# Two weight sums by accumulating loads, the residual by stores, and VectorE's order as written in memory attention

## The chip, the core and the metric

The kernel runs on one core of a Trainium2 chip. TensorE multiplies, VectorE (DVE) and ScalarE (ACT) work on tiles, GpSimd (POOL) and SyncE (SP) mostly issue transfers; each engine takes its own instructions, and semaphores order them against one another. The metric is the device time of one execution in microseconds (us).

## The reference

One layer of a streaming encoder in float32: 512 tokens of width 2048. A normalised input feeds one wide projection; its columns go to a gated short convolution, to latent attention with 16 heads, to cross-attention into 256 memory tokens with 4 heads of width 256, and to the gates. The three branches are projected, gated, merged, put through an output projection and added to the input:

```python
h = rms_norm(x, norm_g[l])
proj = h @ w_in[l]
...
o_conv = (conv_y * jax.nn.silu(conv_z)) @ w_conv_out[l]
...
o_mla = (mla_y * jax.nn.silu(mla_z)) @ w_mla_out[l]
mem_y = memory_attention(mem_q, mem, mem_norm_g[l], w_mem_kv[l], mem_qn_g[l], mem_kn_g[l])
o_mem = (mem_y * jax.nn.silu(mem_z)) @ w_mem_out[l]
merged = (jax.nn.sigmoid(g_conv) * o_conv + jax.nn.sigmoid(g_mla) * o_mla
          + jax.nn.sigmoid(g_mem) * o_mem)
x = x + merged @ w_o[l]
```

Memory attention is, for each head, a softmax over the 256 memory tokens of 512 queries and its product with the values.

## The kernel before

**Number format.** A float32 product is made of three matmuls: each operand is split into a high half (ScalarE copies it, `whi`, L281) and a low half (VectorE subtracts, `wlo`, L282), and `mm3` issues high by high (L161), high by low (L162) and low by high (L163). L163 is the only one that reads a weight's low half, so it is where TensorE waits for `wlo`.

**Panels.** The large projections are done in panels of two 128-column blocks with seven block products in place of eight (PRODUCTS). A panel takes four chunks of weights. A chunk is a 512 KB load of four 128x256 blocks into a `raw` tile of eight (`pair_weights`, four tiles in turn); VectorE then makes four more blocks, as sums: two at once (L276, 128x512), then one (L277) and one (L278), each from the one before; then come the two halves over seven blocks. One chunk feeds 42 matmuls of 256 columns. After the fourth chunk ScalarE copies one result and VectorE combines the products into the panel's four results (L318 to L327 in `panel_steps`), and `finish` does with them what the panel is for. The first two panels go alternately: chunks 0, 1, 2 of panel 0, then of panel 1, then chunk 3 of each.

**Preparation ahead.** `take()` hands the next chunk to the matmuls. `begin(at, stage)` moves a job of the queue on: stage 1 issues the load, 2 the adds, 3 the halves. With each `take`, the chunk itself and the next are brought to stage 3, the one after to stage 2, the one after that to stage 1. `fills` holds small pieces of other work, one run per `take`.

**What sets the order.** TensorE's order and SyncE's are as written. The other engines' order is set by a planner, except where VectorE is put under a manual schedule, and then it takes the instructions as they are written. Before, this holds from step 27 of the memory key and value projection until six panel steps of the input projection are through (`manual_dve`), and again around the turn into the output projection. Every engine takes its own queue in order.

**Places that the change touches.** The input projection begins at about 100 us. In memory attention (`mem_attend`, near 1650 to 1690 us) a head's 512 queries come in two halves; for each half TensorE makes scores, VectorE their maximum (L1152), ScalarE the exponentials with their sums (L1159), VectorE the reciprocals (L1162), and ScalarE scales (L1164). Then TensorE transposes the scaled tiles (L363), ScalarE and VectorE split them (`pt`), and TensorE multiplies with the values (`mv`). The keys of a head are split into `mk0h`, `mk1h` and the low halves. The four heads and other matmuls are interleaved by ORDER_MEM, a string of turns. The output projection takes the last 200 us: the merged branches come back from DRAM (`mg`), get sums and halves, and eight panels with the weights `w_o` end in `finish_o`, which loads the input block (`xr`), adds it on VectorE (L1350) and stores 256 KB from ScalarE's queue.

Of the kernel before, what the change touches and what calls it, by code (L numbers as in the profile page):

```python
# [30 lines left out]
P = 128  # L31
# [54 lines left out]
GATES.update({("gmem", _i): 16 + _i for _i in range(8)})  # L86

# [20 lines left out]
def body(ctx, tc, a, out):  # L108
# [110 lines left out]
    def pair_job(src):  # L219
        return lambda: pair_weights(src)  # L220
# [49 lines left out]
    def pair_weights(src):  # L270
# [3 lines left out]
        nc.sync.dma_start(flat(f[:, 0:4]), src)  # L274
        yield
        vec.tensor_tensor(out=f[:, 4:6], in0=f[:, 1:3], in1=f[:, 0:1].to_broadcast([P, 2, 256]), op=ALU.add)  # L276
# [53 lines left out]
    def panels(xp, weight, n, make, finish, first="acc", tail=None):  # L330
# [3 lines left out]
        order = [(0, c) for c in range(3)] + [(1, c) for c in range(3)] + [(0, 3), (1, 3)]  # L334
        order += [(i, c) for i in range(2, n) for c in range(4)]
        upcoming(*[pair_job(weight[i][c]) for i, c in order])
# [193 lines left out]
    work = panels(xp, a["w_h"], len(SEQUENCE), lambda n: make(n), lambda n, e: finish(n, e), "aux")  # L530
# [54 lines left out]
    begin(2, 2)  # L585
# [175 lines left out]

    def make(n):
        return etile(), None
# [57 lines left out]
    for _ in range(6):  # L821
        next(work)
# [15 lines left out]
    PLACES = ((2, 3), (6, 7), (4, 5), (0, 1))  # L838
# [292 lines left out]
    def mem_attend(head):  # L1131
# [11 lines left out]
        pr = []  # L1143
        for i2 in range(2):
# [16 lines left out]
            ri = pq.tile([P, 2], F32, tag="ri", name="ri", bufs=2)  # L1161
            vec.reciprocal(ri, sm)  # L1162
            for ii in range(2):
                act.activation(p[:, ii], p[:, ii], AF.Copy, scale=ri[:, ii:ii + 1])  # L1164
# [24 lines left out]
    run(ORDER_MEM, w=conv, **{str(n): m[n] for n in range(4)})  # L1189
# [99 lines left out]
    def sums_out(n):  # L1289
        pair_sums(mgs[n])  # L1290

    def split_out(n):
# [11 lines left out]
                 29: ((sums_out, 4),), 30: ((split_out, 4), (merged, 6)), 31: ((sums_out, 5),),  # L1304
                 32: ((split_out, 5),)}
# [9 lines left out]
    for tag, width in (("acc", 512), ("aux", 512), ("acc", 512), ("aux", 256), ("aux", 256)):  # L1315
        if done == 7:
            work = panels(xp, a["w_o"], 8, lambda n: make_o(n), lambda n, e: finish_o(n, e),
                          tail=lambda b, e: tail_o(b, e))
# [19 lines left out]
    def make_o(n):  # L1338
        def middle():
            xrs[n] = pe.tile([P, 2, S], F32, tag="xr", name="xr", bufs=2)  # L1340
# [110 lines left out]
```

## Time and profile before

| | us |
|---|---|
| median of three runs | 2166.34 (2165.52 to 2167.77) |
| the profiled execution | 2162.43 |
| its span in the trace | 2160.7 |
| TensorE matmuls busy | 2122.6 |
| VectorE busy | 1728.2 |
| ScalarE busy | 1010.8 |
| GpSimd busy | 130.9 |

The trace is of one execution. Its span begins at the first recorded instruction, and times below are counted from there. "Busy" is time in which an engine works on an instruction; the idle time of TensorE is the difference from the span. A wait is shown with the engine and line that ended it.

### The profile page before, as it was taken

The numbers are of one execution on the slowest core, as the hardware profiler recorded it, in microseconds if no ns is written. First come the engines' busy times: TensorE is split into PE (matmuls) and PEld (weight loads), VectorE is DVE, ScalarE is ACT, GpSimd is POOL, SyncE is SP. The second block draws the span as 40 slices with busy tenths as digits, with TensorE's granted clock in tenths as the row PEclk, the third lists the DMA queues.
The fourth block names the chain that finished last, engine by engine and source line by source line (L and its number), as shares of the span: only waits on it lengthen the run. The fifth ranks groups of instructions, "written<-read, shape, count | busy, mean of one in ns | idle before, by whom it ended". The sixth has DMA issues, their size and how long they took to land.

```text
span 2160.7 us, 38707 instructions
## 1 busy us (share of the span) xinstructions
PE 2122.6 (98%) x16040; PEld 2037.7 (94%) x16040; DVE 1728.2 (80%) x2740; ACT 1010.8 (47%) x1235; POOL 130.9 (6%) x189
## 2 busy tenths in 40 slices
PE   9989999999999999999999999999999999999899
PEld 7889999999999999999999999898988899987899
DVE  5986878888888888888878876788886688856886
ACT  6743444444444344344444444777765533323333
POOL 0000000000000000000000000212111100011000
PEclk9999999999999999999999999999999999999999
DMA  8634443333333333343444336222346957667443
GB/s 330 248 98 137 158 135 128 128 127 128 127 127 127 125 125 126 126 136 133 137 137 142 131 129 241 90 104 81 112 158 245 355 203 208 201 213 199 141 162 107
DMA packets 93441, 338.51 MB, mean 157 GB/s; under 512 B 10896, under 2 KB 11152, under 8 KB 91216
## 3 DMA queue, kind: packets, MB, share of 16 engines
q1 hardware_dynamic: 70848, 252.58, 34.5%
q0 software_dynamic: 13920, 59.51, 8.6%
q10 hardware_dynamic: 8496, 23.94, 3.1%
q8 instruction: 125, 2.05, 0.4%
q14 instruction: 52, 0.43, 0.1%
HBM read 273.34 MB, written 62.65 MB: 156 GB/s over the span
## 4 chain that ended last, share of the span: by engine, by line
PE 84%; DVE 5%; ACT 2%; DMA 2%; issue 1%; POOL 0%; DVEq 0%; ACTq 0%; POOLq 0%
PE acc L161 14%; PE acc L163 14%; PE acc L162 14%; PE aux L161 13%; PE aux L163 13%; PE aux L162 13%; DVE wlo L282 2%; PE aux L363 1%; PE aux L997 1%; DMA raw<-in_w_h 1%; ACT whi L281 1%; DVE raw L276 0%; PE aux L977 0%; PE aux L980 0%; PE aux L978 0%
## 5 line engine op out<-in xcount | busy, mean ns | idle before, releaser
L281 ACT ACTIVATE whi<-raw 128x1792 fp32r<-128x1792 f32 x304 | 517.6, 1703 | 795.6 <-PE aux L162 336.7
L282 DVE TENSOR_TENSOR wlo<-raw,whi 128x1792 fp32r<-128x1792 f32 x304 | 614.8, 2022 | 204.2 <-ACT whi L281 203.5
L163 PE MATMUL aux<-xp,wlo 128*128 128x256 f32 (+1 forms) x1712 | 479.8, 280 | 6.3 <-DVE wlo L282 6.2
L161 PE MATMUL aux<-xp,whi 128*128 128x256 f32 (+1 forms) x1712 | 480.4, 281 | 0.0
L162 PE MATMUL aux<-xp,whi 128*128 128x256 f32 (+1 forms) x1712 | 479.2, 280 | 0.0
L163 PE MATMUL acc<-xp,wlo 128*128 128x256 f32 x1680 | 470.2, 280 | 3.4 <-DVE wlo L282 3.4
L161 PE MATMUL acc<-xp,whi 128*128 128x256 f32 x1680 | 470.8, 280 | 0.0
L162 PE MATMUL acc<-xp,whi 128*128 128x256 f32 x1680 | 469.6, 280 | 0.0
L163 PEld LDWEIGHTS aux<-xp,wlo 128*128 128x128 f32 (+1 forms) x1712 | 321.1, 188 | 7.5 <-DVE wlo L282 7.5
L161 PEld LDWEIGHTS aux<-xp,whi 128*128 128x128 f32 (+1 forms) x1712 | 320.6, 187 | 0.0
L163 PEld LDWEIGHTS acc<-xp,wlo 128*128 128x128 f32 x1680 | 316.0, 188 | 4.6 <-DVE wlo L282 4.6
L162 PEld LDWEIGHTS aux<-xp,whi 128*128 128x128 f32 (+1 forms) x1712 | 320.2, 187 | 0.0
L161 PEld LDWEIGHTS acc<-xp,whi 128*128 128x128 f32 x1680 | 315.6, 188 | 0.0
L162 PEld LDWEIGHTS acc<-xp,whi 128*128 128x128 f32 x1680 | 315.1, 188 | 0.0
L276 DVE TENSOR_TENSOR raw<-raw 128x512 f32<-128x512 f32 x304 | 208.3, 685 | 36.5 <-DMA raw<-in_w_h 31.8
L155 DVE TENSOR_TENSOR wlo<-raw,whi 128x1024 fp32r<-128x1024 f32 (+2 forms) x89 | 100.5, 1131 | 75.1 <-ACT whi L154 72.7
L154 ACT ACTIVATE whi<-raw 128x1024 fp32r<-128x1024 f32 (+2 forms) x89 | 87.7, 986 | 101.4 <-PE acc L162 43.3
L278 DVE TENSOR_TENSOR raw<-raw 128x256 f32<-128x256 f32 x304 | 127.9, 422 | 6.3
L277 DVE TENSOR_TENSOR raw<-raw 128x256 f32<-128x256 f32 x304 | 127.9, 422 | 5.7
L161 PE MATMUL acc<-whi,blk 128*128 128x384 f32 (+1 forms) x224 | 84.2, 376 | 0.0
L356 POOL TENSOR_TENSOR rs_r<-rs_t,mhalf 128x2 f32<-128x2 f32 (+2 forms) x71 | 65.2, 929 | 276.7 <-DVE rs_t L355 217.2
L163 PE MATMUL acc<-whi,blk 128*128 128x384 f32 (+1 forms) x224 | 80.9, 361 | 0.0
(360 smaller groups left out, 3896.7 us busy)
## 6 DMA issues: line engine op xcount, KB each, us to landing
raw<-in_w_h SPq DMA_DIRECT2D x240, 512.0 KB, 3.5
raw<-in_w_mla_out SPq DMA_DIRECT2D x32, 512.0 KB, 4.2
raw<-in_w_o SPq DMA_DIRECT2D x32, 512.0 KB, 3.6
raw<-in_w_mem_kv SPq DMA_DIRECT2D x31, 512.0 KB, 7.4
gdram<-e ACTq DMA_DIRECT2D x22, 512.0 KB, 2.9
raw<-in_w_ukv SPq DMA_DIRECT2D x16, 512.0 KB, 4.3
raw<-in_w_conv_out SPq DMA_DIRECT2D x16, 512.0 KB, 8.3
aadram<-z POOLq DMA_DIRECT2D x8, 896.0 KB, 3.9
```

The source lines that it names most:

```text
L154: act.activation(hi[:, cols], raw[:, cols], AF.Copy)
L155: vec.tensor_tensor(out=lo[:, cols], in0=raw[:, cols], in1=r32(hi[:, cols]), op=ALU.subtract)
L161: nc.tensor.matmul(o, lhsT=s[0], rhs=m[0], start=start, stop=False, skip_group_check=shared)
L162: nc.tensor.matmul(o, lhsT=s[0], rhs=m[1], start=False, stop=False, skip_group_check=shared)
L163: nc.tensor.matmul(o, lhsT=s[1], rhs=m[0], start=False, stop=stop, skip_group_check=shared)
L276: vec.tensor_tensor(out=f[:, 4:6], in0=f[:, 1:3], in1=f[:, 0:1].to_broadcast([P, 2, 256]), op=ALU.add)
L277: vec.tensor_tensor(out=f[:, 6], in0=f[:, 5], in1=f[:, 1], op=ALU.add)
L278: vec.tensor_tensor(out=f[:, 7], in0=f[:, 6], in1=f[:, 3], op=ALU.add)
L281: act.activation(hi, f[:, 1:8], AF.Copy)
L282: vec.tensor_tensor(out=lo, in0=f[:, 1:8], in1=r32(hi), op=ALU.subtract)
L356: pool.tensor_tensor(out=r, in0=t, in1=mhalf[:, :n], op=ALU.pow)
L363: nc.tensor.transpose(out=b[:, i * P:(i + 1) * P], in_=s, identity=ident)
```

## The change

1. The first eight chunks of the input projection and of the output projection come as 768 KB loads, in which the host has put the first block twice more behind the four blocks; then GpSimd issues a DMA that adds 256 KB of the chunk onto these two (`accum_op`). For these chunks the VectorE instruction L276 is gone; L277 and L278 stay. This takes host arrays `w_h6` and `w_o6`.
2. Before the input projection, the third chunk is begun to stage 1, no longer to stage 2.
3. VectorE's written order holds through nine panel steps, no longer six; the `finish` of panels 0 and 1 runs as fills.
4. The residual: SyncE copies the first seven input blocks from DRAM to the output in DRAM during panels 12 to 18 of the input projection, and `finish_o` adds a panel's result there with one accumulating DMA of GpSimd (512 KB). Only the last panel keeps `xr`.
5. In `mem_attend` the scaling is split off (`scaled`): that of the first half comes after the exponentials of the second, that of the second half just ahead of the first transposes. ORDER_MEM runs with VectorE in its written order.
6. Two pairs of places for blocks in SBUF are swapped, and `split_out(5)` runs as a fill of the output panels.

The core of the diff:

```diff
+FIRST = [(0, c) for c in range(3)] + [(1, c) for c in range(3)] + [(0, 3), (1, 3)]
+SIX = 8
...
-    def pair_weights(src):
+    def pair_weights(src, six):
         f = raw_tile()
-        nc.sync.dma_start(flat(f[:, 0:4]), src)
-        yield
-        vec.tensor_tensor(out=f[:, 4:6], in0=f[:, 1:3], in1=f[:, 0:1].to_broadcast([P, 2, 256]), op=ALU.add)
+        if six is not None:
+            nc.sync.dma_start(flat(f[:, 0:6]), six)
+            nc.gpsimd.dma_start(flat(f[:, 4:6]), src[:, 256:768], accum_op=ALU.add)
+        else:
+            nc.sync.dma_start(flat(f[:, 0:4]), src)
+        yield
+        if six is None:
+            vec.tensor_tensor(out=f[:, 4:6], in0=f[:, 1:3], in1=f[:, 0:1].to_broadcast([P, 2, 256]), op=ALU.add)
         vec.tensor_tensor(out=f[:, 6], in0=f[:, 5], in1=f[:, 1], op=ALU.add)
         vec.tensor_tensor(out=f[:, 7], in0=f[:, 6], in1=f[:, 3], op=ALU.add)
...
-    work = panels(xp, a["w_h"], len(SEQUENCE), lambda n: make(n), lambda n, e: finish(n, e), "aux")
+    work = panels(xp, a["w_h"], len(SEQUENCE), lambda n: make(n),
+                  lambda n, e: fills.append(lambda: finish(n, e)) if n < 2 else finish(n, e), "aux",
+                  six=a["w_h6"])
...
-    begin(2, 2)
+    begin(2, 1)
...
     def make(n):
+        if n >= 12 and n < 19:
+            nc.sync.dma_start(out_rows(n - 12), a["xT"][:, n - 12].rearrange("p (f n) -> p f n", f=2))
...
-    for _ in range(6):
+    for _ in range(9):
         next(work)
     manual_dve.close()
...
+        def scaled(p, sm):
+            ri = pq.tile([P, 2], F32, tag="ri", name="ri", bufs=2)
+            vec.reciprocal(ri, sm)
+            for ii in range(2):
+                act.activation(p[:, ii], p[:, ii], AF.Copy, scale=ri[:, ii:ii + 1])
+                pr.append(p[:, ii])
...
-            ri = pq.tile([P, 2], F32, tag="ri", name="ri", bufs=2)
-            vec.reciprocal(ri, sm)
-            for ii in range(2):
-                act.activation(p[:, ii], p[:, ii], AF.Copy, scale=ri[:, ii:ii + 1])
-                pr.append(p[:, ii])
+            waiting.append((p, sm))
+            if i2 == 1:
+                scaled(*waiting[0])
             yield
         pts = []
         for j in range(2):
+            if j == 0:
+                scaled(*waiting[1])
...
-    run(ORDER_MEM, w=conv, **{str(n): m[n] for n in range(4)})
+    with tc.manual_schedule(engines={DVE}):
+        run(ORDER_MEM, w=conv, **{str(n): m[n] for n in range(4)})
...
     def finish_o(n, e):
-        fills.append(lambda: result(n, e))
...
-            vec.tensor_tensor(out=xr[:, f], in0=two(e)[:, f], in1=xr[:, f], op=ALU.add)
-            nc.scalar.dma_start(out[(2 * n + f) * P:(2 * n + f + 1) * P], xr[:, f])
+        nc.gpsimd.dma_start(out_rows(n), two(e), accum_op=ALU.add)
```

The order of TensorE's matmuls is the same before and after. In the changed kernel L276 to L278 are L288 to L290, L282 is L294, and L1164 is L1171.

**VectorE at chunks 6 to 8 of the input projection.** A `raw` number names one chunk's tile: counted from 0, raw_1208, raw_1261 and raw_1312 are chunks 6, 7 and 8 in both kernels, raw_1364 and raw_1428 are chunks 9 and 10 before, and raw_1489 is chunk 11 now. `e` is the panel's result tile. Before:

```order
L282 TENSOR_TENSOR wlo_1306<-raw_1208,whi_1305 128x1792
L276 TENSOR_TENSOR raw_1261<-raw_1261 128x512
L278 TENSOR_TENSOR raw_1364<-raw_1364 128x256
L277 TENSOR_TENSOR raw_1261<-raw_1261 128x256
L278 TENSOR_TENSOR raw_1261<-raw_1261 128x256
L276 TENSOR_TENSOR raw_1428<-raw_1428 128x512
L277 TENSOR_TENSOR raw_1428<-raw_1428 128x256
L282 TENSOR_TENSOR wlo_1358<-raw_1261,whi_1357 128x1792
L318 TENSOR_TENSOR e_1027<-aux_1029,e_1027 128x2x256
L278 TENSOR_TENSOR raw_1428<-raw_1428 128x256
```

Now:

```order
L294 TENSOR_TENSOR wlo_1357<-raw_1261,whi_1356 128x1792
L288 TENSOR_TENSOR raw_1312<-raw_1312 128x512
L289 TENSOR_TENSOR raw_1312<-raw_1312 128x256
L290 TENSOR_TENSOR raw_1312<-raw_1312 128x256
L330 TENSOR_TENSOR e_1025<-aux_1027,e_1025 128x2x256
L335 TENSOR_TENSOR e_1025<-aux_1028,e_1025 128x512
L288 TENSOR_TENSOR raw_1489<-raw_1489 128x512
L336 SCALAR_TENSOR_TENSOR e_1025<-aux_1028,e_1025 128x256
L338 TENSOR_TENSOR e_1025<-aux_1029,e_1025 128x256
L339 TENSOR_TENSOR e_1025<-aux_1029,e_1025 128x256
L294 TENSOR_TENSOR wlo_1414<-raw_1312,whi_1413 128x1792
```

Before, adds of chunk 10 (raw_1428) stood ahead of the low half of chunk 7 (raw_1261). Now the low halves of the first eight chunks have no later chunk's L276 ahead of them, and the combining of panel 0 stands whole ahead of the low half of the ninth chunk.

**ScalarE in memory attention**, from the exponentials of head 0 to the first scaling of the third head. `p` numbers name the halves: 18712, 18737, 18781, 18806 are 0A, 0B, 1A, 1B before; 18721, 18742, 18786, 18807 now. Before:

```order
L130 ACTIVATE mk0h_18894<-mkr_18890 128x256
L1159 ACTIVATE p_18712,sm_18711<-aux_18694,nm_18709,mqs_98 128x256 x2
L1159 ACTIVATE p_18737,sm_18736<-aux_18719,nm_18734,mqs_98 128x256 x2
L130 ACTIVATE mv_18682<-mvr_18680 128x512
L1164 ACTIVATE p_18712<-p_18712,ri_18715 128x256 x2
L1159 ACTIVATE p_18781,sm_18780<-aux_18763,nm_18778,mqs_98 128x256 x2
L130 ACTIVATE mv_18687<-mvr_18685 128x512
L1164 ACTIVATE p_18737<-p_18737,ri_18740 128x256 x2
L1159 ACTIVATE p_18806,sm_18805<-aux_18788,nm_18803,mqs_98 128x256 x2
L1164 ACTIVATE p_18781<-p_18781,ri_18784 128x256 x2
L130 ACTIVATE pt0_18833<-aux_18828 128x512
```

Now:

```order
L136 ACTIVATE mk0h_18903<-mkr_18899 128x256
L136 ACTIVATE mk1h_18907<-mkr_18899 128x256
L1190 ACTIVATE p_18742,sm_18741<-aux_18724,nm_18739,mqs_98 128x256 x2
L1171 ACTIVATE p_18721<-p_18721,ri_18745 128x256 x2
L136 ACTIVATE mv_18689<-mvr_18687 128x512
L136 ACTIVATE mv_18694<-mvr_18692 128x512
L1190 ACTIVATE p_18786,sm_18785<-aux_18768,nm_18783,mqs_98 128x256 x2
L1190 ACTIVATE p_18807,sm_18806<-aux_18789,nm_18804,mqs_98 128x256 x2
L1171 ACTIVATE p_18786<-p_18786,ri_18810 128x256 x2
L1171 ACTIVATE p_18742<-p_18742,ri_18829 128x256 x2
L136 ACTIVATE pt0_18838<-aux_18833 128x512
L136 ACTIVATE pt1_18846<-aux_18841 128x512
```

The scaling of 0B has moved from ahead of 1B's exponentials to behind them and behind the scaling of 1A.

**GpSimd in the output projection** (after; no row of L283 and L1378 stood there before):

```order
L1312 DMA mg_21723<-mgdram_117 128x1024
L283 DMA raw_21857<-in_w_o 128x512
L1319 DMA mgdram_117<-gt_21276 128x1024
L1312 DMA mg_21825<-mgdram_117 128x1024
L283 DMA raw_21893<-in_w_o 128x512
L283 DMA raw_21947<-in_w_o 128x512
L1312 DMA mg7_21880<-mgdram_117 128x1024
L283 DMA raw_22001<-in_w_o 128x512
L1378 DMA out_0<-e_21882 128x2x512
```

The accumulating loads of the weights stand between the stores (`mgdram<-gt`) and loads (`mg<-mgdram`) of the merge, in GpSimd's one queue.

More of the change, by code (lines that the diff above doesn't have):

```diff
@@ L328, in panel_steps, with panels @@
         yield
[L330 to L336, printed above, removed]
+    def panels(xp, weight, n, make, finish, first="acc", tail=None, six=None):
+        order = FIRST + [(i, c) for i in range(2, n) for c in range(4)]
+        upcoming(*[pair_job(weight[i][c], six[at] if six is not None and at < SIX else None)
+                   for at, (i, c) in enumerate(order)])
         tags = (first, "aux" if first == "acc" else "acc")
@@ L760, in body, with out_rows @@
     conv_e = {}
+    def out_rows(n):
+        return out[2 * n * P:2 * (n + 1) * P].rearrange("(f p) n -> p f n", f=2)
     def make(n):
+        if n >= 12 and n < 19:
+            nc.sync.dma_start(out_rows(n - 12), a["xT"][:, n - 12].rearrange("p (f n) -> p f n", f=2))
         return etile(), None
@@ L1143, in mem_attend @@
         pr = []
+        def scaled(p, sm):
[4 more added lines that the diff above has]
+                pr.append(p[:, ii])
+        waiting = []
         for i2 in range(2):
@@ L1303, in body @@
                  25: ((split_out, 3), (merged, 4), (merged, 5), (gate_load, 7)),
-                 29: ((sums_out, 4),), 30: ((split_out, 4), (merged, 6)), 31: ((sums_out, 5),),
-                 32: ((split_out, 5),)}
+                 29: ((sums_out, 4),), 30: ((split_out, 4), (merged, 6)), 31: ((sums_out, 5),)}
     late_blocks = []
@@ L1317, in body @@
             work = panels(xp, a["w_o"], 8, lambda n: make_o(n), lambda n, e: finish_o(n, e),
-                          tail=lambda b, e: tail_o(b, e))
+                          tail=lambda b, e: tail_o(b, e), six=a["w_o6"])
         banks = [bank(tag) for _ in range(width // P)]
@@ L1339, in middle @@
         def middle():
-            xrs[n] = pe.tile([P, 2, S], F32, tag="xr", name="xr", bufs=2)
-            nc.sync.dma_start(xrs[n].rearrange("p f n -> p (f n)"), a["xT"][:, n])
+            if n == 7:
+                xrs[n] = pe.tile([P, 2, S], F32, tag="xr", name="xr", bufs=1)
+                nc.sync.dma_start(xrs[n].rearrange("p f n -> p (f n)"), a["xT"][:, n])
         return pe.tile([P, 8, H], F32, tag="e", name="e", bufs=2), middle
     def finish_o(n, e):
-        fills.append(lambda: result(n, e))
-    def result(n, e):
-        xr = xrs[n]
-        for f in range(2):
-            vec.tensor_tensor(out=xr[:, f], in0=two(e)[:, f], in1=xr[:, f], op=ALU.add)
-            nc.scalar.dma_start(out[(2 * n + f) * P:(2 * n + f + 1) * P], xr[:, f])
+        nc.gpsimd.dma_start(out_rows(n), two(e), accum_op=ALU.add)
     def tail_o(b, e):
@@ L1367, in body @@
     merged(7)
-    fills += [lambda: None, lambda: sums_out(6), lambda: split_out(6), lambda: sums_out(7), lambda: split_out(7)]
+    fills += [lambda: split_out(5), lambda: sums_out(6), lambda: split_out(6), lambda: sums_out(7), lambda: split_out(7)]
     for n, _ in enumerate(work):
@@ L1437, in layout @@
     a["w_o"] = np.stack([halved(i["w_o"][0], c, c + P) for c in range(0, D, 256)])
+    for name in ("w_h", "w_o"):
+        first = np.stack([a[name][i][c] for i, c in FIRST[:SIX]])
+        a[name + "6"] = np.ascontiguousarray(np.concatenate([first, first[:, :, :256], first[:, :, :256]], axis=2))
     return a
```

6 lines of the change are left out of this document (3 added, 3 removed).

## The prediction, made before the changed kernel ran

> **What bounds the kernel now.** I read the busy shares first, then the busy time by stretch of the span, then what TensorE waited for. The columns of the second view are: stretch, length, then busy time of TensorE's matmuls, its weight loads, VectorE, ScalarE and GpSimd, the granted clock, the DMA share and GB/s.
>
> ```profile
> PE 2122.6 (98%) x16040; PEld 2037.7 (94%) x16040; DVE 1728.2 (80%) x2740; ACT 1010.8 (47%) x1235; POOL 130.9 (6%) x189
> ```
> ```profile
> 20.00:114.00 94.00, 91.57 (x449) 76.20 (x447) 75.18 (x94) 67.89 (x89) 6.26 (x8) 1.00 0.78 284
> 114.00:155.00 41.00, 33.83 (x275) 32.61 (x276) 34.55 (x42) 16.18 (x13) 0.00 (x0) 1.00 0.28 90
> 155.00:1160.00 1005.00, 1003.88 (x8512) 1003.02 (x8511) 835.29 (x1174) 422.57 (x327) 14.62 (x20) 1.00 0.40 131
> 1650.00:1690.00 40.00, 37.38 (x202) 31.06 (x202) 27.75 (x57) 27.52 (x70) 6.26 (x12) 0.96 0.71 254
> 1945.00:2050.00 105.00, 93.27 (x612) 83.83 (x611) 83.25 (x111) 37.57 (x30) 8.34 (x13) 1.00 0.57 171
> 2050.00:2150.00 100.00, 100.00 (x852) 100.00 (x851) 82.15 (x110) 35.98 (x25) 0.00 (x0) 1.00 0.42 143
> ```
>
> TensorE is the bound: of 2160.7 us it is idle for 38.1, and no edit here takes a matmul away. The idle time sits in spots: 41.00 − 33.83 = 7.2 us at the start of the input projection and 105.00 − 93.27 = 11.7 at the turn into the output projection. In the long stretches between (1.1 us idle in 1005, none in the last 100 us of output panels) VectorE has slack, and work taken from it buys nothing. So the question is only what the edits do to these spots, and whether they open new ones.
>
> TensorE's waits (engine, line, releaser; total us, times, longest), of the stretches 20 to 170, 1945 to 2050 and 1650 to 1690 us:
>
> ```profile
> PE aux L163 <- DVE wlo L282: 5.4, 3, 3.0
> PE acc L163 <- DVE wlo L282: 3.4, 4, 1.4
> ...
> PE acc L163 <- DVE wlo L282: 9.8, 7, 2.6
> PE aux L163 <- DVE wlo L282: 1.0, 4, 0.2
> ...
> PE aux L363 <- ACT p L1164: 2.4, 3, 1.7
> ```
>
> The first spot waits 8.8 us and the second 10.8 us for the low half of a weight chunk (wlo), the last of five operations on a chunk; the third spot, memory attention, waits 2.4 us for a scaled softmax tile. These 22 us are what the change can touch.
>
> **Input projection.** The costs of one chunk, and VectorE's own timeline where it goes wrong (start us, duration, then idle before it and the releaser):
>
> ```profile
> L281 ACT ACTIVATE whi<-raw 128x1792 fp32r<-128x1792 f32 x304 | 517.6, 1703 | 795.6 <-PE aux L162 336.7
> L282 DVE TENSOR_TENSOR wlo<-raw,whi 128x1792 fp32r<-128x1792 f32 x304 | 614.8, 2022 | 204.2 <-ACT whi L281 203.5
> L276 DVE TENSOR_TENSOR raw<-raw 128x512 f32<-128x512 f32 x304 | 208.3, 685 | 36.5 <-DMA raw<-in_w_h 31.8
> L278 DVE TENSOR_TENSOR raw<-raw 128x256 f32<-128x256 f32 x304 | 127.9, 422 | 6.3
> ```
> ```profile
> 142.47 0.69 DVE L276 TENSOR_TENSOR raw<-raw 128x512 f32<-128x512 f32 x1 [3.01 <-DMA raw<-in_w_h]
> 143.20 0.42 DVE L277 TENSOR_TENSOR raw<-raw 128x256 f32<-128x256 f32 x1
> 143.54 2.02 DVE L282 TENSOR_TENSOR wlo<-raw,whi 128x1792 fp32r<-128x1792 f32 x1
> ...
> 149.13 0.69 DVE L276 TENSOR_TENSOR raw<-raw 128x512 f32<-128x512 f32 x1 [1.84 <-DMA raw<-in_w_h]
> ```
>
> A chunk is 42 matmuls, at 1003.88 us / 8512 = 0.118 us each 4.95 us of TensorE, against 0.69 + 2 × 0.42 + 2.02 = 3.55 us of VectorE. The chunk rate is no trouble; the wlo of 143.54 was late because VectorE takes its queue in order and stood 3.01 us at a later chunk's L276, whose data had not landed. That cost TensorE the longest wait, 3.0; the 1.84 at 149.13 does the same once more.
>
> The change takes eight L276 away (8 × 0.685 = 5.5 us of VectorE), begins chunk 2's adds after wlo of chunk 1, and keeps VectorE's written order through nine panel steps, so wlo of chunks 6 and 7 no longer stands behind later chunks' adds. Walking the queue with the durations above: of the seven waits, those at chunks 1, 5, 6 and 7 (counted from 0) go and about 1 us stays at chunks 2 and 4. But the same written order now puts the combining of panel 0 (about 3 us: two 128x512 forms, three 128x256, and a copy) after wlo(7) and ahead of wlo(8), and the combining of panel 1, the scaling of panel 0 and the adds of two further chunks ahead of wlo(9). Panel 0 ends with chunk 6. Counted from there, wlo(8) is ready about 5.6 us later where chunk 8 asks at 5.1 (late by 0.5), and wlo(9) at 13 to 15 where chunk 9 asks at 10.5 (late by 2.5 to 4.5); chunk 10 then waits about 1. So 8.8 goes down to about 5 or 6; a wait also sits in gaps this view doesn't name (41.00 − 33.83 is 7.2 us in one stretch alone). I take **−5**; bounds −8.8 (nothing new waits) and 0 (the new waits equal the old).
>
> **Its price: two landings in series.** GpSimd adds 256 KB of the chunk into the loaded tile, which can start only when the 768 KB load has landed; L277 then waits for GpSimd's queue. An accumulating load is not in the trace. The nearest rows (KB of one transfer, median us from issue to landing):
>
> ```profile
> raw<-in_w_h SPq DMA_DIRECT2D x240, 512.0 KB, 3.5
> mgdram<-sg POOLq DMA_DIRECT2D x8, 512.0 KB, 5.6
> mgdram<-gt POOLq DMA_DIRECT2D x8, 512.0 KB, 6.3
> mgdram<-kn POOLq DMA_DIRECT2D x4, 256.0 KB, 9.5
> ```
>
> The rows of 5.6 and 6.3 are accumulating stores, twice the bytes; the last is GpSimd's slowest plain one. From below a plain load's 3.5 bounds it, from above 9.5. I take 6. A slot of the four raw tiles comes free at wlo(n − 4): 3.5 + 6 + 0.85 (L277, L278) + 1.70 (whi) + 2.02 (wlo) = 14.1 us, within 4 × 4.95 = 19.8. So it is hidden, until the accumulation alone takes 19.8 − 8.1 = 11.7. The Trainium skill ("DMA: Bandwidth & Descriptors", rules for kernel authors) says that an accumulating transfer must wait for the earlier one's semaphore, because nothing holds the bytes between its read and its write; so the landings cannot overlap, which the sum above has by the kernel's own wait, and no run so far shows an accumulating load.
>
> **Output projection.** Eight more L276 leave, 5.5 us, and in the second spot four of the L1350 adds (128x512, as L276: 2.7 us); split_out(5) moves from the tail of the merge to a panel's fill. VectorE is busy 83 of 105 us there, in order, and 10.8 us are waits for wlo. Removed work can cut at most 8.2 of it. Not all arrives: the remaining chunks' L288 (the former L276) still stands ahead of earlier wlo, waiting for loads, as at 142.47; and here the eight accumulations lie in GpSimd's queue behind merge stores and loads. I take **−6**, bounds −8.2 and 0. The other ten of the 14 adds, the ScalarE stores and seven input loads lie under 100 us of full TensorE (the row of 2050): 0. Should that cover fail, it is 10 × 0.685 = 6.9 us of VectorE more in hand, never less. The seven DRAM-to-DRAM copies (512 KB) fall in stretches at DMA share 0.40: 0.
>
> **Memory attention.** Here nothing is removed; the written VectorE order and the deferred scaling move work. ScalarE and TensorE before:
>
> ```profile
> 1655.49 0.42 ACT L130 ACTIVATE mk0h<-mkr 128x256 fp32r<-128x256 f32 x1 [2.35 <-PE aux L163]
> ...
> 1656.18 0.55 ACT L1159 ACTIVATE p<-aux,nm,mqs 128x256 f32<-128x256 f32 x1
> ...
> 1658.34 0.63 ACT L130 ACTIVATE mv<-mvr 128x512 fp32r<-128x512 f32 x1
> 1658.86 0.91 ACT L1164 ACTIVATE p<-p,ri 128x256 f32<-128x256 f32 x2
> 1659.66 0.56 ACT L1159 ACTIVATE p<-aux,nm,mqs 128x256 f32<-128x256 f32 x1
> ...
> 1661.27 0.91 ACT L1164 ACTIVATE p<-p,ri 128x256 f32<-128x256 f32 x2
> ...
> 1664.90 0.93 ACT L1164 ACTIVATE p<-p,ri 128x256 f32<-128x256 f32 x2
> 1665.70 1.07 ACT L154 ACTIVATE whi<-raw 128x1024 fp32r<-128x1024 f32 x1
> 1666.64 1.09 ACT L130 ACTIVATE pt<-aux 128x512 fp32r<-128x512 f32 x2
> ...
> 1682.00 0.56 ACT L1159 ACTIVATE p<-aux,nm,mqs 128x256 f32<-128x256 f32 x1
> ```
> ```profile
> 1659.42 0.73 PE L363 MATMUL aux<-ident,p 128*128 128x128 f32 x2 [0.18 <-ACT p L1164]
> 1661.83 1.17 PE L363 MATMUL aux<-ident,p 128*128 128x128 f32 x6 [1.68 <-ACT p L1164]
> ...
> 1664.98 2.05 PE L363 MATMUL aux<-ident,p 128*128 128x128 f32 x8
> ...
> 1681.55 1.03 PE L363 MATMUL aux<-ident,p 128*128 128x128 f32 x8
> ```
>
> Call the softmax halves of head h hA and hB. ScalarE's queue was: mk (head 3), exps 0A and 0B, scale 0A, exps 1A, scale 0B (1661.27), exps 1B, scale 1A, two pt, scale 1B. Now 0A's exps come before mk, but mk still waits for head 1's scores at 1655.49, with 0B's exps behind it (1656.2 to 1657.3), then scale 0A, two mv (0.6 each at most), four exps (0.55 each), scale 1A, and only then 0B: 1657.3 + 0.9 + 1.2 + 2.2 + 0.9 = 1662.5 for its start, against 1661.27. Head 0's transposes wait about 1 us longer. Scale 1B now stands behind 0B (0.9), two pt (1.1), a weight half (1.07) and two mv (1.2): 1662.5 + 4.3 = 1666.8 and, as the second pt waits for head 0's late transposes, rather 1667.5, against 1664.90; head 1's transposes at 1664.98 wait about 3. Scale 2B moves behind head 3's four exps (the last at 1682.00) and scale 3A: about 1683.4, where TensorE asked at 1681.55 and did not wait; and by VectorE's order head 3's maxima stand behind head 1's products, so 2 to 4.5. Sum: +6 to +8.5. I take **+8.5**, since each wait also delays the queue that the next one stands in; bounds 0 (ScalarE's slack absorbs it) and +10.
>
> **The clock.** In two stretches TensorE ran at half clock:
>
> ```profile
> 171.69:175.10 3.41, 3.41 (x18) 3.41 (x18) 2.70 (x7) 0.00 (x0) 0.54 (x1) 0.50 0.64 231
> 1663.31:1666.72 3.41, 3.41 (x12) 2.44 (x11) 1.44 (x3) 3.41 (x8) 0.00 (x0) 0.50 0.43 163
> ```
>
> Each loses half of 3.41 = 1.7 us, after a wait of 1.7 beside transposes. Three longer waits could bring one or two more (+1.7 to +3.4), fewer waits at 170 could take one away; I put +1.5. The Trainium skill ("TensorE: Matmul & The Clock Gate", Part 1 and "Why this matters for your kernels") wants no idle gap above about 3 us, and its Part 4 has transposes not counted as busy. The trace agrees with the second more than with the first, having a gated window after a gap of 1.7. By the first alone the clock term would be about 0, by both together up to +3.4, which speaks against this change.
>
> **The sum** is −5 − 6 + 8.5 + 1.5 = −1. The profiled execution took 2162.43 us (span 2160.7, 1.7 around it), 3.9 below the median of 2166.34. 2162.4 − 1 = 2161.4, and with the same 3.9 the median comes to **2165.3**, no change that can be measured: 0.2%, or 4.3 us, is about what a measurement of this kernel can tell.
>
> **The rivals.**
> - *Memory attention stays cheap.* If ScalarE takes 0B and 2B where the data is ready, as its 47% share would let it were its queue not fixed, the +8.5 falls to +1 and the clock term to 0: −5 − 6 + 1 = −10, 2156. For it: 27.5 of 40 us busy on ScalarE, so there is room. Against: the queue is in order, and 0B's exps were held by mk already at 1655.49. Chance 0.27, with mixtures below −4.3.
> - *The accumulating loads land late (slower).* Place: L289, the former L277, in VectorE's in-order queue. It decides from 11.7 us of landing, above the 9.5 of the slowest row. At 16 us a cycle of four chunks takes 24.1 for 19.8, 1.1 per chunk; four chunks at each projection are paced so (the first four are prefetched): +8.6, or 2174. For it: one GpSimd queue that also waits for merge loads, and the first 114 us at a DMA share of 0.78. Against: both accumulating rows are near 6. Chance 0.13.
> - *Memory attention at its bound with two more half-clock windows*, and the projections at half their gains: +10 + 3.4 − 5.5 = +7.9, 2174. It decides where each wait of 3 us falls inside one window. For it: the row of 1663.31. Against: both gains must fail at once. Chance 0.10.
> - *The edits don't act* (L289 and L288 take the place of L276, wait for wait; the new order is as good as the old): 0, 2166; within the forecast.
>
> **How the numbers follow.** The forecast, −4.3 to +4.3 with its middle at −1, gets 0.50; of it 0.02 falls out above and 0.01 below. Faster: 0.27 + 0.01 = 0.28. Slower: 0.13 + 0.10 + 0.02 = 0.25. Within 0.2%: 0.47. The likeliest case has 2161 to 2170; to hold 8 of 10 the range takes in the first rival to its value and most of the two slower ones: 2156 to 2174.
>
> **What would show it.** Right: no wait above 1 us for wlo before chunk 8, then one of 2 to 4.5 at chunk 9; transposes (L363) waiting 6 us or more in total on the scale of 0B, 1B and 2B, with four exps directly ahead of it in ScalarE's timeline; accumulating loads landing in 5 to 9 us; total idle of TensorE within 3 us of 38. Wrong: L363 waits near 2.4 as before (then the first rival), or L289 with idle time ended by GpSimd's DMA and a DMA landing above 11 us (then the second). A time wrong by more than 5 us means one of the three spots moved by twice its term.

## The result, and the profile after

The changed kernel took 2175.28 us (median of 6 runs, 2171.81 to 2179.10), the kernel before beside it 2165.70 (2163.70 to 2167.77): +9.6 us, ratio 1.0047 with a 95% interval of 1.0035 to 1.0059. It is slower; the forecast was −1 us and no change, with a range that ended at 2174. The profiled execution took 2179.1 us (span 2177.2), the slowest of the six, so differences between the two profiles are larger than that of the medians.

The busy shares, then the busy time by stretch, columns as before:

```profile
PE 2131.8 (98%) x16040; PEld 2047.5 (94%) x16040; DVE 1711.0 (79%) x2710; ACT 1012.9 (47%) x1235; POOL 154.0 (7%) x212
```
```profile
114.00:155.00 41.00, 40.09 (x340) 39.89 (x339) 35.73 (x47) 20.58 (x17) 3.50 (x4) 1.00 0.59 164
...
1650.00:1690.00 40.00, 29.92 (x152) 25.25 (x150) 19.68 (x41) 23.16 (x60) 3.74 (x7) 0.87 0.52 178
...
1945.00:2050.00 105.00, 99.74 (x609) 88.78 (x607) 76.10 (x97) 39.85 (x32) 18.56 (x24) 0.98 0.75 202
2050.00:2150.00 100.00, 93.97 (x775) 93.76 (x776) 76.99 (x103) 33.89 (x23) 5.98 (x5) 0.97 0.49 130
```

The first row already splits the loss. The same 16040 matmuls kept TensorE busy for 2131.8 us, not 2122.6: 9.2 us more, which the stretches of half clock below can account for. Idle time is 2177.2 − 2131.8 = 45.4 us, not 38.1: 7.3 us more of waiting. Together 16.5, the difference of the spans. The idle time left the start of the input projection (0.9 us in the first stretch, was 7.2), and came up in memory attention (10.1, was 2.6) and in the last 100 us (6.0, was none).

Where the clock was half in the changed kernel, most of these stretches (before there were two; one that opens in the last 3 us of either span, when TensorE has finished, is left out):

```profile
110.80:114.20 3.40, 3.40 (x18) 3.40 (x18) 3.24 (x2) 2.79 (x3) 0.87 (x1) 0.50 0.82 270
168.90:172.30 3.40, 3.40 (x18) 3.40 (x17) 1.75 (x5) 0.00 (x0) 0.00 (x0) 0.50 0.56 169
1660.50:1663.90 3.40, 3.40 (x11) 2.78 (x12) 1.77 (x4) 1.47 (x3) 0.00 (x0) 0.50 0.61 243
1667.30:1674.10 6.80, 6.26 (x18) 4.99 (x19) 3.18 (x5) 2.08 (x4) 0.00 (x0) 0.50 0.00 0
...
2001.80:2005.20 3.40, 3.40 (x18) 3.40 (x18) 2.67 (x5) 1.70 (x1) 1.44 (x2) 0.50 0.79 223
2053.00:2059.80 6.80, 5.25 (x24) 5.26 (x25) 3.43 (x6) 1.70 (x1) 1.05 (x1) 0.50 0.73 152
```

With two more, at 1691.2 and 1759.5, they are ten windows of 3.41 us. The Trainium skill ("TensorE: Matmul & The Clock Gate", Part 1) has a window of 3413 ns that runs freely; the length agrees. The Trainium skill (the same page, "Why this matters for your kernels") has a rule of no idle gap above about 3 us. This case goes below it: a wait of 1.56 us that ended at 109.56 stood ahead of the first window, one of 1.92 that ended at 1759.26 of another. Not every such wait brings a window: behind 1.70 us at 114.04 in the kernel before and 1.60 us at 1747.17 in the changed one there is none. And the window at 168.9 follows no wait but 32 matmuls of a single column each, 3.6 us by the profile.

What TensorE waited for, whole span:

```profile
PE acc L169 <- DVE wlo L294: 13.2, 7, 5.7
PE aux L376 <- ACT p L1171: 10.7, 3, 4.0
PE aux L169 <- DVE wlo L294: 7.1, 5, 3.3
```

The scaled softmax tiles are waited for 10.7 us, was 2.4. The waits for `wlo` (a weight's low half) hold 20.3 us in 12 times, was 21.8 in 22: fewer and longer.

The start of the same matmul in the two profiled executions gives the loss by stage. Positive is later than before; the column names the matmul by its time in the kernel before:

| kernel | 150 | 1170 | 1375 | 1648 | 1720 | 1760 | 1984 | 2035 | 2070 |
|---|---|---|---|---|---|---|---|---|---|
| the change | −4.8 | −3.0 | −2.6 | −2.6 | +9.7 | +13.4 | +15.4 | +11.0 | +16.2 |

It gains 3 us in the input projection, loses 12.2 in memory attention and 3.7 just behind it, 2.0 more by 1984, gains 4.3 over the first output panels and gives back 5.2 right after.

### The profile page after: what moved, and what is told of

It reads as the page before. It is cut to its first block, busy times and chain, and to the rows that moved or that the text cites. A ratio compares the mean times of both kernels' runs of the same rounds, so it can differ in the third digit from the quotient of the medians.

```text
span 2177.2 us, 38715 instructions
## 1 busy us (share of the span) xinstructions
PE 2131.8 (98%) x16040; PEld 2047.5 (94%) x16040; DVE 1711.0 (79%) x2710; ACT 1012.9 (47%) x1235; POOL 154.0 (7%) x212
## 4 chain that ended last, share of the span: by engine, by line
PE 77%; issue 7%; DMA 7%; DVE 5%; ACT 3%; POOL 1%; SPq 0%; POOLq 0%; DVEq 0%; ACTq 0%
PE acc L168 13%; PE acc L167 13%; PE acc L169 13%; PE aux L168 11%; PE aux L167 11%; PE aux L169 11%; DVE wlo L294 1%; DMA raw<-in_w_h 1%; DMA mgdram<-gt 1%; DMA mgdram<-sg 1%; PE aux L1019 1%; DMA raw<-in_w_o 1%; PE aux L376 1%; DMA mg<-mgdram 1%; DMA sb<-gdram 1%
## 5 line engine op out<-in xcount | busy, mean ns | idle before, releaser
L294 DVE TENSOR_TENSOR wlo<-raw,whi 128x1792 fp32r<-128x1792 f32 x304 | 614.6, 2022 | 205.4 <-ACT whi L293 204.6
L288 DVE TENSOR_TENSOR raw<-raw 128x512 f32<-128x512 f32 x288 | 197.1, 684 | 48.4 <-DMA raw<-in_w_h 28.6
L290 DVE TENSOR_TENSOR raw<-raw 128x256 f32<-128x256 f32 x304 | 127.8, 421 | 6.6
```

Of the source, the lines that this page charges most:

```text
L290: vec.tensor_tensor(out=f[:, 7], in0=f[:, 6], in1=f[:, 3], op=ALU.add)
L294: vec.tensor_tensor(out=lo, in0=f[:, 1:8], in1=r32(hi), op=ALU.subtract)
```

## The experiments

Ratios are against the kernel before, run beside on the same chip; the differences in us are against its median there (2163.48 to 2164.70; the runs come from four chips). "Stage" numbers are starts of the same matmul in profiled executions, as in the table.

### Memory attention as before, all else changed (2161.28)

```diff
-            waiting.append((p, sm))
-            if i2 == 1:
-                scaled(*waiting[0])
+            ri = pq.tile([P, 2], F32, tag="ri", name="ri", bufs=2)
+            vec.reciprocal(ri, sm)
+            for ii in range(2):
+                act.activation(p[:, ii], p[:, ii], AF.Copy, scale=ri[:, ii:ii + 1])
+                pr.append(p[:, ii])
...
-    with tc.manual_schedule(engines={DVE}):
-        run(ORDER_MEM, w=conv, **{str(n): m[n] for n in range(4)})
+    run(ORDER_MEM, w=conv, **{str(n): m[n] for n in range(4)})
```

> The changed kernel with the memory attention of before (scaling in place, VectorE's order there from the planner); all else of the change stays. Theory A (memory attention and the half-clock windows that its waits bring cost most of the loss): transposes wait about 2.4 us again in place of 10.7, the half-clock windows between 1640 and 1700 us fall from 4 to 1, and the median falls by 10 to 13 us, to 2162 to 2166. Theory B (the loss sits at the turn into the output projection, and what is lost in memory attention would be lost behind it anyway): it falls by less than 5, to 2171 or more.

Measured: 2161.28, before 2164.08, −2.8; ratio 0.9989 (0.9979 to 0.9998). Without its memory attention the change is a small gain; with it a loss of 9.6. Theory A holds: the fall is 12.4. In the stretch of 1640 to 1700 us the scaled tiles are waited for 3.3 us, and no half-clock window lies there.

### Memory attention alone (2177.87)

The new `mem_attend` and the written order of VectorE there, put into the kernel before.

> The kernel before with the new memory attention alone (deferred scaling, written VectorE order there). Theory A: +9 to +13 us against before, 2175 to 2179, with three waits of 3 to 4 us before transposes and three or more extra half-clock windows. Theory B: under +4.

Measured: +13.8; ratio 1.0069 (1.0054 to 1.0084). It is slightly more than expected. Stages: −0.3 at 1648, +11.4 at 1720, +15.2 at 1760, +15.8 at the end. Nothing of the loss is absorbed behind it, and 3.7 us of it arise only after the section, at the start of the attention output projection (waits for `wlo` there of 1.6 and 1.9 us, with a half-clock window behind the second).

### Which half of it: written order alone (2171.30), deferred scaling alone (2167.37)

```diff
-            waiting.append((p, sm))
-            if i2 == 1:
-                scaled(*waiting[0])
+            scaled(p, sm)
...
-            if j == 0:
-                scaled(*waiting[1])
```
```diff
-    with tc.manual_schedule(engines={DVE}):
+    if True:
```

> The changed kernel with the scaling in memory attention in its old place (right behind its own exponentials), while VectorE's written order stays there. If the deferred scaling is what makes the transposes wait: 2.4 to 5 us of such waits in place of 10.7, and 2162 to 2168. If the written order of VectorE is the cause (it sets where ScalarE's inputs are ready): waits of 9 us or more stay, 2173 to 2178.

> The other half: the scaling deferred as in the change, VectorE's order in memory attention left to the planner. If the deferred scaling is the cause: 8 us or more of waits before transposes, 2171 to 2178. If the written order is: 2.4 to 5 us and 2162 to 2168.

Measured: +7.8, ratio 1.0035 (1.0022 to 1.0048), and +3.9, ratio 1.0022 (1.0012 to 1.0032). TensorE's waits between 1640 and 1700 us, of the written order alone and then of the deferred scaling alone:

```profile
PE aux L376 <- ACT p L1171: 6.8, 5, 1.8
PE aux L167 <- ACT p L1190: 0.5, 1, 0.5
```
```profile
PE aux L376 <- ACT p L1171: 6.9, 3, 3.6
```

Neither half is *the* cause: by the waits, 6.8 and 6.9 us, both runs fall between the two outcomes that were expected. Against the −2.8 with the old memory attention the written order costs about 10.6, the deferral about 6.7, both together 12.4: they overlap. By stage from 1648 to 1760: +8.1, +5.7, and +16.0 for both.

The same place in the changed kernel shows why. ScalarE's timeline, at heads 0 and 1 and at head 2:

```profile
1658.54 0.56 ACT L1190 ACTIVATE p<-aux,nm,mqs 128x256 f32<-128x256 f32 x1
...
1659.08 1.69 ACT L1171 ACTIVATE p<-p,ri 128x256 f32<-128x256 f32 x4
...
1667.28 0.91 ACT L1171 ACTIVATE p<-p,ri 128x256 f32<-128x256 f32 x2 [0.97 <-DVE ri L1169]
...
1688.77 0.55 ACT L1190 ACTIVATE p<-aux,nm,mqs 128x256 f32<-128x256 f32 x1
...
1689.31 1.69 ACT L1171 ACTIVATE p<-p,ri 128x256 f32<-128x256 f32 x4
```
```profile
1660.43 1.73 PE L376 MATMUL aux<-ident,p 128*128 128x128 f32 x6 [3.50 <-ACT p L1171]
...
1667.84 1.73 PE L376 MATMUL aux<-ident,p 128*128 128x128 f32 x6 [3.21 <-ACT p L1171]
...
1690.66 1.64 PE L376 MATMUL aux<-ident,p 128*128 128x128 f32 x6 [4.02 <-ACT p L1171]
```

Each of the three runs of transposes waits 3.2 to 4.0 us for a scaled tile, in heads 0 and 2 the third. Ahead of that one in ScalarE's queue stand the next head's four exponentials and a scaling, which it does not need. Head 1 is different: ahead of its scaling at 1667.28 stand two `pt`, a weight half and two `mv`, and ScalarE itself then stands 0.97 us for VectorE's reciprocal. With the deferral alone head 1's transposes do not wait (the waits of 6.9 us are 3.57 and 3.12 at heads 0 and 2, and 0.18), so this part comes with the written order.

### More busy matmuls in the waits (2176.59)

```diff
             b = bank("aux")
+            if j == 0:
+                for _ in range(10):
+                    nc.tensor.matmul(b[:, :P], lhsT=ident, rhs=ident, start=True, stop=True)
```

> The changed kernel with ten more matmuls (128x128, of the identity, results overwritten) on TensorE ahead of each head's first transposes in memory attention, so that part of the wait is busy. If the half-clock windows there come of the waits: the waits end when they ended, one to three of the four windows between 1640 and 1700 us go, and the time falls by 2 to 5 us, to 2170 to 2173. If they don't: four windows stay, and the time is the same or up to 4 us longer.

Measured: 2176.59 (12 runs, 2155.39 to 2180.52), ratio 1.0051 (1.0033 to 1.0070), before 2164.08. By the median nothing is gained, where 2 to 5 us were expected. The stretch of 1650 to 1675 us, with the extra matmuls and then in the changed kernel:

```profile
1650.00:1675.00 25.00, 22.59 (x139) 19.57 (x138) 12.30 (x27) 15.80 (x38) 2.41 (x5) 1.00 0.57 211
```
```profile
1650.00:1675.00 25.00, 18.28 (x78) 14.91 (x77) 11.42 (x23) 14.67 (x36) 1.61 (x3) 0.80 0.46 170
```

The three windows there are gone (granted clock 1.00 for 0.80), that at 1691 stays. From 1645 to 1700 us the profiled execution is 1.5 us faster than the change's, though it does 40 matmuls more. So these three windows do come of the waits, as far as one execution shows; what they cost cannot be read from the time, which scatters over 25 us here.

### The output projection without the accumulating weight loads (2182.36)

```diff
-                          tail=lambda b, e: tail_o(b, e), six=a["w_o6"])
+                          tail=lambda b, e: tail_o(b, e))
```

> The changed kernel, but the first eight chunks of the output projection come as before, with the added pair of sums on VectorE; those of the input projection keep the accumulating loads. If the accumulating loads there gained what the eight first panels show (about 5 us less up to 2040 us): 4 to 6 us slower than the change, 2179 to 2181. If they only moved the wait to the chunks behind (5.9 us at 2054): within 2 us of the change, 2173 to 2177.

Measured: +18.3 against before, ratio 1.0094 (1.0077 to 1.0111), so about 9 slower than the change (+9.6). It is beyond what was expected. Its profiled execution was the fastest of its six (2177.5), so the stages do not show the whole of it: −1.0 from 1984 to 2035, where the change has −4.3. The accumulating loads gain; that they only move the wait is against this run. How much they gain it does not settle: other pairs of runs give less (below).

### The written order kept longer in the output projection (2165.57)

```diff
-        if n == 8:
+        if n == 16:
             manual_dve.close()
```

with the old memory attention; what it is compared with is that kernel's −2.8.

> The changed kernel with the memory attention of before, and VectorE's written order in the output projection kept through 16 panel steps in place of 8. In the change the ninth and tenth chunks' low halves stand behind pair sums (L288) of later chunks whose loads had not landed (4.0 us each). If that order is what makes the waits of 4.8 and 2.8 us there: they fall to 2 us in sum and the time is 3 to 6 us below that of the change with the old memory attention alone (2161.3), 2155 to 2158. If the late loads hold the chunks whatever the order: the waits stay at 6 us or more and the time at 2160 to 2163.

Measured: +2.1, ratio 1.0015 (1.0006 to 1.0024): 5 us worse, against both theories. VectorE's pair sums that stood still behind the new end of the written order:

```profile
2066.30 0.69 DVE L288 TENSOR_TENSOR raw<-raw 128x512 f32<-128x512 f32 x1 [1.98 <-DMA raw<-in_w_o]
...
2083.42 0.69 DVE L288 TENSOR_TENSOR raw<-raw 128x512 f32<-128x512 f32 x1 [4.88 <-DMA raw<-in_w_o]
```

The waits did not go, they moved with the end of the written order: at 2035 us this kernel is 8.8 us ahead of before, at 2070 9.8, at 2100 2.3 behind. TensorE waits 1.56, 2.01 and 4.70 us on the way, and 6.8 us of half clock begin at 2085.8. What costs, by these rows, is the passage from the written order, where a chunk's sums come late, to the planner's, where they come early and ahead of an earlier chunk's low half. No run tests this reading by itself.

### Old memory attention and old residual (2157.28)

`make_o`, `finish_o` and `result` as before, without the copies from DRAM to DRAM.

> The changed kernel with the memory attention of before and with the residual as before (input blocks loaded, added on VectorE, stored by ScalarE's queue). The weight loads beside an accumulating store of a panel landed in 7.3 and 5.9 us, where their median is 3.7. If those stores make the loads late: loads back below 5 us, the waits at the ninth and tenth chunks down by 3 us or more, and 2156 to 2160. If not: the 14 adds come back onto VectorE for nothing, 2161 to 2165.

Measured: −6.2; ratio 0.9972 (0.9959 to 0.9984). It is faster than both kernels, by 3.4 than the same with the new residual. As expected of late loads, the slowest weight load there lands in 4.6 us, no longer 6.2, and TensorE's two longest waits are 2.4 and 2.0 us in place of 4.7 and 2.7.

### The residual alone (2168.81)

The copies in DRAM and the accumulating stores, put into the kernel before.

> The kernel before with the residual part alone: copies in DRAM and accumulating stores in place of loads, 14 adds and stores. The prediction's term was 0. By the pair of runs with and without it under the old memory attention it costs 4: expected +2 to +5, with weight loads beside a store landing in 5 us and more. If the cost needs the accumulating weight loads beside it: 0 to +1.

Measured: +5.1; ratio 1.0025 (1.0014 to 1.0036), at the upper end of what was expected, and without any accumulating weight load beside it. By stage it all comes between 2035 and 2070 (+1.1, then +4.9). GpSimd's stores there, then VectorE's longest wait for a load between 2025 and 2062 us before, and the two longest now:

```profile
2032.08 1.22 POOL L1368 DMA_DIRECT2D out<-e  x1 [33.03 <-DVE e L339]
2041.79 1.19 POOL L1368 DMA_DIRECT2D out<-e  x1 [8.49 <-DVE e L339]
```
```profile
2028.96 0.69 DVE L276 TENSOR_TENSOR raw<-raw 128x512 f32<-128x512 f32 x1 [0.64 <-DMA raw<-in_w_o]
```
```profile
2039.80 0.69 DVE L288 TENSOR_TENSOR raw<-raw 128x512 f32<-128x512 f32 x1 [2.75 <-DMA raw<-in_w_o]
...
2048.90 0.69 DVE L288 TENSOR_TENSOR raw<-raw 128x512 f32<-128x512 f32 x1 [3.54 <-DMA raw<-in_w_o]
```

The slowest weight load between 2025 and 2062 us lands in 6.0 us (before: 4.9; in the change 7.3; with the old residual in the change 4.6). A load delayed by 1 to 3 us just behind a store holds VectorE's queue, in which an earlier chunk's low half stands behind the sums. VectorE stands 8.9 us for loads in this stretch, was 2.1.

TensorE's waits do not add up to more by that. From 1984 to 2100 us they are 10.3 us, and 11.3 before; but they come in longer pieces (longest 4.7 us, was 2.6), and behind the longest lie 6.8 us of half clock, from 2042.7. The same stretch before, and now:

```profile
2025.00:2062.00 37.00, 30.33 (x253) 29.52 (x252) 32.96 (x52) 10.86 (x8) 0.00 (x0) 1.00 0.41 143
```
```profile
2025.00:2062.00 37.00, 29.50 (x222) 28.68 (x220) 27.09 (x41) 9.27 (x8) 2.41 (x2) 0.91 0.41 100
```

TensorE is busy for almost as long and gets through 31 fewer matmuls. The copies in DRAM and the stores were not tested apart; the copies come far ahead, in panels 12 to 18 of the input projection, and at 2035 us this run is only 1.1 us behind.

### The input projection alone (2168.29), and with the swapped places (2161.24)

The accumulating loads of `w_h`, `begin(2, 1)`, nine steps and the deferred finishes in the kernel before; the second run also has

```diff
-    PLACES = ((2, 3), (6, 7), (4, 5), (0, 1))
+    PLACES = ((2, 3), (4, 5), (6, 7), (0, 1))
```

> The kernel before with the input projection's part of the change alone: accumulating loads, chunk 2 begun a stage less, nine panel steps in written order, two finishes as fills. The prediction's term was -5 us. The profile of the whole change shows -3, half of the gain being lost at a late first chunk, at chunks 8 and 9 and in more half-clock windows: expected -1 to -3. At -4 or less the term was right; at 0 or more the part is worth nothing.

> The input projection's part alone again, now with the two swapped pairs of block places that the change has too (without them: 2168.3, with TensorE waiting 4.0 us at 1358 us for a block whose load was issued at 1350 where it had been issued at 1343). If the old places made that wait by holding the load behind the input part's later ends: no wait there, and 2159 to 2163 against a kernel before at about 2164. If the input part makes it by itself: the wait stays, 2166 to 2169.

Measured: +4.5, ratio 1.0025 (1.0013 to 1.0037), a miss; and with the places −3.5, ratio 0.9982 (0.9970 to 0.9994). SyncE's issues, without and with the swap, and TensorE's wait without it:

```profile
1350.23 1.55 SPq L868 DMA_DIRECT2D blk<-latdram  x2
```
```profile
1340.20 0.80 SPq L868 DMA_DIRECT2D blk<-latdram  x2
```
```profile
PE acc L167 <- DMA blk<-latdram: 4.0, 1, 4.0
```

Without the swap the last two blocks of the attention's input are loaded later, TensorE waits 4.0 us for one, and 6.8 us of half clock follow: 7.2 us between 1340 and 1375 by stage. Taken from the +4.5 they leave −2.7, near the other run. The profiled execution without the swap, the slowest of its twelve, does not show that gain: it is 3.4 us behind already at 1345.

### The places alone (2172.81), and with the output part (2166.74)

> The kernel before with the swapped block places alone. If they matter only together with the input part: no difference to before, 2162 to 2166. If they gain by themselves: 2 us or more below before.

> The output projection's part alone with the swapped block places (without them 2164.3, no gain against before). If the places matter only together with the input part: 2162 to 2166 as without. If they gain by themselves: 2157 to 2161.

Measured: +8.1, ratio 1.0033 (1.0021 to 1.0045), and +2.0, ratio 1.0017 (1.0006 to 1.0028). Both expectations missed: in these two the swap brings the wait on, 4.2 and 4.3 us for `blk<-latdram`, again with 6.8 us of half clock. So the swap gains nothing by itself; it goes with the input part. Old with old and new with new have no wait, either mixture costs about 7 us. Why the load is held in the mixtures was not followed up.

### The output part alone (2164.27)

> The kernel before with the output projection's accumulating loads alone (and the second half of a block split moved into a panel's fill). The prediction's term for this was -6 us against before, 2157 to 2160 with a kernel before at 2163 to 2166. If the accumulating loads only move the wait to the chunks behind them: 0 to -2.

Measured: +0.5; ratio 1.0003 (0.9993 to 1.0013), places as before. By the time it is worth nothing; by stage it gains 4.6 between 1984 and 2035 in its profiled execution, as the run with the swap does (4.8) and as the change does (4.3). That execution was 4 us behind already at 150 us, with a half-clock window at 12.9 us where nothing was changed. The profiled executions of the input projection alone (without the swap) and of the places alone have one at 12.8 and 12.7 us too. Whether all of their runs have it is open.

### Accumulating loads from the third chunk on (2157.74)

> The changed kernel with the memory attention and the residual of before (2157.3), and with chunks 0 and 1 of the input projection loaded as before, so that only chunks 2 to 7 there have accumulating loads. In the change the first chunk's accumulating load was issued at 97.3 us and VectorE stood 3.5 us for it. If that late landing costs the 2 to 2.5 us by which chunk 0 starts later: no such wait, and 2154 to 2156. If VectorE's order is what delays chunk 0: 2157 to 2159.

Measured: −6.0; ratio 0.9975 (0.9962 to 0.9988), the same as with all eight (−6.2). In the change VectorE stood 3.52 us for the first accumulation:

```profile
104.70 0.43 DVE L289 TENSOR_TENSOR raw<-raw 128x256 f32<-128x256 f32 x1 [3.52 <-DMA raw<-in_w_h]
```

Here that wait is gone, and its profiled execution is 4.8 us better at 150 us than that with all eight loads (−7.6 and −2.8). The medians do not show it, so by them the second outcome (2157 to 2159) came.

## Why the prediction was wrong

The parts, put together one on the other, each by its difference to the kernel before beside it:

| part | forecast | measured | from |
|---|---|---|---|
| input projection (with the places) | −5 | −3.5 | alone with the places |
| output projection, weight loads | −6 | −2.7 | −6.2 less −3.5 |
| residual by stores | 0 | +3.4 | −2.8 less −6.2 |
| memory attention, clock | +8.5, +1.5 | +12.4 | +9.6 less −2.8 |
| sum | −1 | +9.6 | |

The rows are differences of one chain of runs, so that they add up shows nothing. Each alone, the four are −3.5, +0.5, +5.1 and +13.8, or +15.9 in sum. And the intervals reach 2 to 4 us to either side, so by these times −3.5 and −2.7 cannot be told from the forecasts −5 and −6. The stages can be compared over all profiled executions. From 1984 to 2100 us, mean difference to before (number of executions):

| | old residual | residual by stores |
|---|---|---|
| output sums on VectorE | +0.2 (5) | +3.6 (2) |
| accumulating weight loads | −3.4 (4) | +0.8 (5) |

The run with the longer written order is left out. So the loads gain 2.8 to 3.6 us and the stores cost 3.4 to 4.2, with either choice of the other.

- **Input projection: mechanism right, size in doubt.** Chunks 1, 5, 6 and 7 lost their waits as walked, and new waits of about 1 and 3.3 us stand at chunks 8 and 9 (0.5 and 2.5 to 4.5 were forecast); the 1 us each at chunks 2, 4 and 10 did not come. Left out was the first chunk, whose accumulation was issued only at 97.3 us and landed 7 us later, and a half-clock window after it. Over the ten profiled executions with this part as it is in the change, the gain between 60 and 1170 us is 1.3 on average (from 3.4 gained to 1.3 lost); the six with the old part, the kernel before among them, lose 0.9. That is 2.2 us in place of 5: by 150 us it is 5.3, and the wait at chunk 9 with what follows takes 3.1 back.
- **The landings: one well priced, one not.** The accumulation took 6.7 us here and 6.0 in the output projection, for the 6 taken. But the load ahead of it was priced at the 3.5 us of a 512 KB load; at 768 KB it took 6.5 and 7.1:

```profile
raw<-in_w_h SPq DMA_DIRECT2D x8, 768.0 KB, 6.5
raw<-in_w_o SPq DMA_DIRECT2D x8, 768.0 KB, 7.1
raw<-in_w_h POOLq DMA_DIRECT2D x8, 256.0 KB, 6.7
raw<-in_w_o POOLq DMA_DIRECT2D x8, 256.0 KB, 6.0
```

  With 6.5 and 6.7 the sum of 14.1 us becomes 17.8, still within the 19.8 of four chunks, but with 2 us to spare and not 5.7.
- **Output projection: too large.** Removed work was credited with 6 of 8.2 us, 2.7 of them for adds that the residual part takes away. The panels in question gain 4.3 to 4.8 by stage up to 2035, and 2.8 to 3.6 up to 2100. With the residual it was −6 in the forecast and is +0.7 by the times (+0.6 by the table of stages): 6.7 of the 10.6 us by which the sum was off.
- **The residual: the step that failed.** "Should that cover fail, it is 10 × 0.685 = 6.9 us of VectorE more in hand, never less" priced only the work taken away. The step brought seven accumulating stores of 512 KB onto the transfers at the place where TensorE already waited for low halves (up to 2.6 us each, before). Loads issued just behind a store landed late, VectorE's queue stood for them (up to 3.5 us, was 0.6), and a longer wait of TensorE was followed by half clock. They cost 3.4 to 5.1 us. The row of 100 us of full TensorE was read as cover for the whole stage, but with the residual alone the first store is issued at 2032, ahead of that row, and in the change TensorE is idle for 6.0 us in it.
- **Memory attention: mechanism right.** The order of ScalarE's queue did what was walked, for heads 0, 1 and 2: waits before transposes of 3.5, 3.2 and 4.0 us, 10.7 in sum, against "6 us or more in total". The waits were sized well: +8.5, where they rose by 8.3. What the sum did not have is the clock on top and 3.7 us behind the section, at the start of the next projection. By stage, from 1648 to 1760 us, the three executions with this section as it is in the change lose 14.0 to 16.0, and the ten with the old one gain 0.1 to 0.6. The rival in which the section costs nothing had 0.27 and was wrong.
- **The clock: put at a sixth of what it cost.** +1.5 was put for one window; there were eight more, and TensorE was 9.2 us longer busy with the same matmuls in the profiled execution. They came after waits of 1.56 us and more in every section that was disturbed, not in memory attention alone; one, at 168.9, came after no wait. The prediction read both windows of the kernel before as following a wait of 1.7 us; that holds for the one at 1663.31, while the one at 171.69 follows a wait of 0.94 us and 32 matmuls of one column. The count of two is itself that of a single execution, 3.9 us below its median; other executions of the kernel before were not traced. The third rival had the right direction (more windows, halved gains, +7.9) with a chance of 0.10.
- **The signs.** A time wrong by more than 5 us was to mean that one of the three spots moved by twice its term. The miss is 10.6, and by the times none did that: it is the residual, which had no term, the clock and two gains that came out smaller. TensorE's total idle time, 45.4 us, left the band of 3 us around 38. And the second rival's 2174 is the forecast of 2165.3 plus 8.6, so it keeps gains that late loads would have taken away.
- **The places** were not priced at all. In the change as it is they cost nothing; wrongly paired they would have cost 7.

The best of the runs keeps the accumulating loads, the input part and the places, and the memory attention and residual of before: 2157.28 us, ratio 0.9972.

## What to carry to other kernels

Where an engine takes its queue in order, ask of a deferred instruction what will stand ahead of it, not how much that engine has to spare; ScalarE was 47% busy and still made TensorE wait 10.7 us. Price a step by what it adds at its worst place too: a transfer "off the path" lies beside the loads that some queue is waiting for. And where TensorE is 98% busy, count a wait of 2 us, and several waits joined into a longer one, with the half-clock window that can follow.

## What was not expected of the hardware

- Half-clock windows of 3.41 us follow waits far shorter than themselves: 1.56 and 1.92 us were enough here, though not every time. The same 16040 matmuls were busy for 2122.6 and for 2131.8 us.
- Accumulating loads of 256 KB into SBUF landed in 6.0 to 6.7 us (median; 3.9 to 9.5), nearly as long as accumulating stores of 512 KB to DRAM (medians 5.6 to 7.4).
- Over all traces, 47 plain loads of 512 KB issued within 3 us behind such a store of a panel landed in 5.1 to 7.3 us (median 5.9); the 310 others between 2025 and 2150 us had a median of 3.6, and three of them took more than 5.3.
- The kernel before itself scatters from 2157 to 2172 us over the runs, and single profiled executions differ by up to 4 us already at 150 us, in stages that no edit touches. Differences between parts below about 3 us are not told apart by the times here.
